# A gated-linear-attention layer: the six level products of a head as 64 by 64 products in one run, and a new order behind the merge

## The chip, the cores and the metric

The kernel runs on one core of one Trainium2 chip. The metric is the device time of one execution in microseconds. Three executions of the kernel before took 2208.63, 2210.24 and 2212.44 us; the median is 2210.24 us.

## The reference

One hybrid decoder layer over 2048 tokens plus 16 learned meta tokens, model width 1024, float32. One input projection feeds two branches, a Mamba-2 state-space branch (SSD, 16 heads in 4 groups, chunks of 128) and gated linear attention (GLA, 4 heads, key width 128, value width 256). The branches are normalised, projected, gated by sigmoids, summed, projected once more and added to the residual; a last RMS norm follows. The change touches only the attention matrix of GLA inside a chunk:

```python
def step(s, inp):                      # one chunk of one GLA head
    qi, ki, vi, gi = inp               # gi: cumulative sum of log gates
    o_inter = einsum('bhtk,bhkv->bhtv', qi * exp(gi), s)
    rel = exp(where(causal, gi[:, :, :, None, :] - gi[:, :, None, :, :], -inf))
    att = einsum('bhtk,bhsk,bhtsk->bhts', qi, ki, rel)
    o_intra = einsum('bhts,bhsv->bhtv', att, vi)
    k_dec = ki * exp(gi[:, :, -1:] - gi)
    s_new = exp(gi[:, :, -1])[..., None] * s + einsum('bhsk,bhsv->bhkv', k_dec, vi)
    return s_new, o_inter + o_intra
```

## The kernel before, in words

**Stages.** The 2048 tokens are four blocks of 512 (`BLK`). For each block the first stage walks through 48 to 49 pieces of projection work on TensorE (PE); most pieces are 24 products of 512 columns or 48 of 256 on PE. After each piece `step()` lets every running generator go one step: `ssd_scan` for the four SSD groups, `gla_scan` for the four GLA heads, `gates`, `fetch_u` for the next block. In this text GLA heads are counted through, 0 to 15, four a block: head 9 is the second head of the third block. A second stage, after all blocks, does the branch and output projections.

**Who sets the order.** In the first stage PE and the DMA queue of SyncE run in program order, written out by hand. VectorE (DVE), ScalarE (ACT) and GpSimd (POOL) are put in order by a scheduler when the kernel is built; on the chip each runs its list in order. `tc.issue_after(x)` is a wish to that scheduler: what is inside comes behind `x` on `x`'s engine. Tiles come from pools: a tag with `bufs=n` has n slots, and a tile has to wait for a slot until the last reader of the tile in it is done.

**One GLA head** (`gla_scan`, L814 on). A chunk of 128 by 128 attention is put together from levels. For the half sizes 64, 32, 16, 8, 4, 2 (`LEVELS`) `level_in` (L847) computes scaled keys and queries: a subtraction on DVE (L858), two exponentials on ACT (L861, L862), and three products on DVE (L863 for the keys, L865 twice for the queries) into the tile `kq`. `level_out` (L869) multiplies them on PE, two products of 128 by 128 (L873), into a PSUM bank of the pool `pc` (two banks), and puts the part that belongs to the level into `xa`: ACT copies the first (L877), DVE copies the others under a mask (L880). The levels of one head are spread over four steps. In step five comes the last level, the sums for the pairs next to each other and the diagonal (L945, PE, by a matrix of ones), and the merge on DVE: L947 under a mask into `xa`, L950 times the triangles into `att`, L953 the diagonal under a mask. In step six PE transposes half of `att` (L960) and `advance(0)` adds the first two chunks to the state: six products on PE, then two updates on DVE (L969). In step seven PE computes the output of chunks 0 and 1 (L981 and three products each), and `advance(2)`, which takes the PSUM bank that `advance(0)` had and so must wait until both updates have read it. The next head begins at step seven of this one, so its levels stand beside them.

In the last block heads 13 and 14 begin closer to each other: head 14 is begun at the end of `proj_v12` (`LATE_G`), and where two scans run in these steps the newer one goes first.

**Slots.** `sq` has six slots (`ex`, `kq` and `att` of GLA, the decay matrices of SSD), `c1` eight, `xd` four.

**SSD's products inside a chunk** (L717) already have the form that the change brings to GLA: stationary 64 columns of `dm`, moving 64 columns of `xdt`, output rows 0 to 63 and 64 to 127 in turn.

Of the kernel before, what the change touches and what calls it, by code (L numbers as in the profile page):

```python
# [8 lines left out]
F32 = mybir.dt.float32  # L9
# [10 lines left out]
BLK = 512  # L20
NCH = BLK // P
# [2 lines left out]
NH = 16  # L24
EPS = 1e-6
NWR = 3
NSQ = 6
NT4 = 5
NACT = 8
NC1 = 8  # L30
NAS = 6
LATE_G = 2
LEVELS = (64, 32, 16, 8, 4, 2)
# [10 lines left out]
def trunk_kernel(ctx: ExitStack, tc: tile.TileContext, xm, xmt, w_feat, w_tok, w_v3, w_zm, w_br, w_o,  # L44
                 cf32, cmsk, pvec, fnw, hvec, gw2, out):
    nc = tc.nc
# [80 lines left out]
    bpool, wk, sm, const = pool1("bpool", 1), pool1("wk", 2), pool1("sm", 4), pool1("const", 1)  # L127
# [4 lines left out]
    pc = ctx.enter_context(tc.tile_pool(name="pc", bufs=2, space=bass.MemoryType.PSUM))  # L132
# [4 lines left out]
    def bank(pool, tag):  # L137
        return mk(pool, [P, 512], F32, tag)
# [5 lines left out]
    tris = cst[:, 2:4, :]  # L144
# [246 lines left out]
    msk = const.tile([P, NMSK, P], U8, name="msk")  # L391
# [225 lines left out]
            feats.append(f)  # L617
            yield

    cbs, evicted, convd = {}, [], []  # L620

    def behind():
        return tc.issue_after(evicted[-1].ins) if evicted else nullcontext()
# [6 lines left out]
    def ssd_scan(o, g):  # L630
# [10 lines left out]
        if m0:  # L641
            ps = bank(pt, "pt")
# [20 lines left out]
                                tri.unsqueeze(1).to_broadcast([P, NCH, P]), op=ALU.mult)  # L663
        yt = mk(wk, [P, NCH, 256], F32, "tok4", bufs=NT4)
        ssq = mk(sm, [P, 4], F32, "ssq")
        held, intra = {}, {}

        def before(c):
            a = m0 + c * P
            ci = ci0 + c  # L670
            if c + 1 < NCH:
                fetch_cb(o, g, c + 1)
            cb = cbs.pop((g, c))
            ps = bank(pt, "pt")
            for j, f in enumerate((x0, x1, bf)):
                nc.tensor.transpose(ps[:, j * P:(j + 1) * P], f[:, a:a + P], ident)
            px = ps[:, :256].rearrange("p (h c) -> p h c", c=64)
            xdt = mk(wk, [P, 4, 64], F32, "xd", bufs=NCH)
            nc.vector.tensor_tensor(xdt, px, hb(tkd[:, ci, hs], P), op=ALU.mult)
            xw = mk(wk, [P, 4, 64], F32, "c1", bufs=NC1)  # L680
            nc.vector.tensor_tensor(xw, px, hb(wde[:, ci, hs], P), op=ALU.mult)
            nc.vector.tensor_tensor(yt[:, c].rearrange("p (h c) -> p h c", c=64), px,
                                    hb(d_skip[:, hs], P), op=ALU.mult)
            bt = mk(wk, [P, P], F32, "bt")
            nc.scalar.activation(bt, ps[:, 256:384], AF.Copy)
            dm = mk(wk, [P, 4, P], F32, "sq", bufs=NSQ)
            with behind() if o.b == 0 else nullcontext():
                for h in range(4):
# [58 lines left out]
        r = rstd_of(ssq, 4, 1.0 / 1024)  # L747
# [63 lines left out]
    def gla_scan(o, h, last=False):  # L811
# [27 lines left out]

        xa = mk(wk, [P, 2, P], F32, "c1", bufs=NC1)
        kqs = {}

        def level_in(half):
            nb = BLK // (2 * half)
            npc = P // (2 * half)  # L847

            def view(t):
                return t.rearrange("p (b two h) -> p b two h", two=2, h=half)  # L850

            def view5(t):
                return t.rearrange("p (r o b two h) -> p r o b two h", o=2, b=npc, two=2, h=half)

            ex = mk(wk, [P, BLK], F32, "sq", bufs=NSQ)
            kq = mk(wk, [P, BLK], F32, "sq", bufs=NSQ)
            ev = view(ex)
            nc.vector.tensor_tensor(  # L858
                ex.rearrange("p (b s) -> p b s", s=2 * half), gr.rearrange("p (b s) -> p b s", s=2 * half),
                view(gr)[:, :, 0, half - 1:half].to_broadcast([P, nb, 2 * half]), op=ALU.subtract)  # L860
            nc.scalar.activation(ev[:, :, 0], ev[:, :, 0], AF.Exp, scale=-ITEMP)  # L861
            nc.scalar.activation(ev[:, :, 1], ev[:, :, 1], AF.Exp, scale=ITEMP)  # L862
            nc.vector.tensor_tensor(view(kq)[:, :, 0], ev[:, :, 0], view(k)[:, :, 0], op=ALU.mult)  # L863
            for i in range(2):
                nc.vector.tensor_tensor(view5(kq)[:, :, 1 - i, :, 1], view5(ex)[:, :, i, :, 1],  # L865
                                        view5(q)[:, :, i, :, 1], op=ALU.mult)
            kqs[half] = kq

        def level_out(half):  # L869
            kq = kqs.pop(half)  # L870
            ps = bank(pc, "pc")
            for r in range(2):
                nc.tensor.matmul(ps[:, r * P:(r + 1) * P], kq[:, 2 * r * P:(2 * r + 1) * P],  # L873
                                 kq[:, (2 * r + 1) * P:(2 * r + 2) * P], start=True, stop=True)
            pv2 = ps[:, :256].rearrange("p (r t) -> p r t", t=P)
            if half == 64:
                nc.scalar.activation(xa, pv2, AF.Copy)  # L877
            else:
                mi = msk[:, LEVELS.index(half)].unsqueeze(1).to_broadcast([P, 2, P])
                nc.vector.copy_predicated(xa, mi, pv2)  # L880

        level_in(64)
        yield
        if m0:
            ps = bank(pt, "pt")
# [12 lines left out]
        if not last:  # L898
            turn_keys()
        level_in(32)  # L900
        level_out(64)
        level_in(16)
        yield
        if m0:
            ps = bank(pt, "pt")
            nc.tensor.matmul(ps[:, :256], btm[:META], s_gla[:META, h], start=True, stop=True)
            nc.vector.tensor_copy(s_gla[:, h], ps[:, :256])
        level_out(32)
        level_in(8)
        level_out(16)  # L910
        level_in(4)
        yield
        level_out(8)
        level_in(2)
        level_out(4)


        def halves(t):
# [18 lines left out]
        yield  # L937
        if last:
            turn_keys()
        level_out(2)  # L940
        sums_ = []
        for hl, n in parts:
            ps = bank(pt, "pt")
            for i in range(2):
                nc.tensor.matmul(ps[:, :n], ones_r, hl[i], start=i == 0, stop=i == 1)  # L945
            sums_.append(ps)
        nc.vector.copy_predicated(xa, msk[:, len(LEVELS)].unsqueeze(1).to_broadcast([P, 2, P]),  # L947
                                  sums_[0][:, :256].rearrange("p (r t) -> p r t", t=P))
        att = mk(wk, [P, NCH, P], F32, "sq", bufs=NSQ)
        nc.vector.tensor_tensor(att.rearrange("p (r o) t -> p r o t", o=2),  # L950
                                xa.unsqueeze(2).to_broadcast([P, 2, 2, P]),
                                tris.unsqueeze(1).to_broadcast([P, 2, 2, P]), op=ALU.mult)
        nc.vector.copy_predicated(att, msk[:, 0].unsqueeze(1).to_broadcast([P, NCH, P]),  # L953
                                  sums_[1].rearrange("p (c t) -> p c t", t=P))
        atp = [beside_64("atp") for _ in range(2)]
        split(*[t[:, 0::2] for t in atp], att[:, 0::2])
        yield
# [548 lines left out]
def _layout(inputs):  # L1506
# [40 lines left out]
    cmsk[:, 0] = np.eye(P)  # L1547
    for i, h in enumerate(LEVELS + (1,)):
        if i:
            cmsk[:, i] = (row // (2 * h) == col // (2 * h)) & (row // h != col // h)  # L1550

    def pcol(v):
        return v.reshape(-1, P).T
# [37 lines left out]
```

## Time and profile before

The profiled execution took 2209.51 us; the trace spans 2207.7 us of it, from the first instruction to the last.

| engine | busy us | share of the span | instructions |
|---|---|---|---|
| PE, matmuls | 2174.5 | 98% | 12301 |
| PEld, weight loads (beside PE) | 1867.9 | 85% | 12301 |
| DVE | 1553.8 | 70% | 2871 |
| ACT | 1188.5 | 54% | 2767 |
| POOL | 693.8 | 31% | 689 |

A row of the timeline reads: start us, duration us, engine, line, operation, out<-in, partitions x elements, count, and in brackets how long the engine was idle before and what it waited for. PE's matmuls overlap each other, so the time that a matmul takes up is the distance between two starts, not its duration. The same holds, by less, on DVE. A float32 matmul stands in the trace as two records.

### The profile page before, as it was taken

To read this page: it belongs to the slowest core of one execution; us is meant where nothing else is said; L and a number is where in the kernel's file an instruction comes from. 1 tells how busy PE (TensorE), PEld (TensorE's weight loads), DVE (VectorE), ACT (ScalarE), POOL (GpSimd) and SP (SyncE) were. 2 spreads that over 40 slices of the span, in tenths; PEclk is the share of its full clock that TensorE was granted. 3 is DMA by queue.
4 is the path that set the end of the run, shared out by engine and by line. 5 is a ranking of instruction groups with operands and counts; after the bars stand their busy time and mean duration, and the time that the engine had idled before them with its cause. 6 is when DMAs were issued, how large, how long until landed. Compare 5 with 4: busy or idle time off the path is not lost.

```text
span 2207.7 us, 35845 instructions
## 1 busy us (share of the span) xinstructions
PE 2174.5 (98%) x12301; PEld 1867.9 (85%) x12301; DVE 1553.8 (70%) x2871; ACT 1188.5 (54%) x2767; POOL 693.8 (31%) x689
## 2 busy tenths in 40 slices
PE   7999999999999999999999999999999999999998
PEld 7999889888888988888988888878888888888887
DVE  5786675677577676658677666674789955789876
ACT  5666655466455456545465554464644545554544
POOL 5444433222222122221222100166233374324341
PEclk9999999999999999999999999999999999999999
DMA  9766775667778677778677664376768866787753
GB/s 316 254 228 235 255 271 211 218 217 244 257 253 265 210 227 230 249 257 274 208 223 238 215 216 161 124 265 214 246 221 297 304 223 216 240 286 255 255 187 121
DMA packets 313702, 518.00 MB, mean 235 GB/s; under 512 B 28080, under 2 KB 162480, under 8 KB 313520
## 3 DMA queue, kind: packets, MB, share of 16 engines
q1 hardware_dynamic: 247008, 419.89, 58.3%
q10 hardware_dynamic: 65872, 93.74, 11.6%
q8 instruction: 96, 1.57, 0.3%
q0 software_dynamic: 640, 2.10, 0.2%
q14 instruction: 86, 0.70, 0.1%
HBM read 368.42 MB, written 147.19 MB: 234 GB/s over the span
## 4 chain that ended last, share of the span: by engine, by line
PE 86%; DVE 4%; ACT 3%; DMA 3%; POOL 1%; issue 1%; SPq 1%; POOLq 0%; ACTq 0%; DVEq 0%
PE pj L223 19%; PE pj L225 19%; PE pj L224 19%; PE pt L225 4%; PE pt L224 4%; PE pt L223 4%; PE pc L223 2%; PE pc L224 2%; PE pc L225 2%; PE pc L873 2%; PE pc L717 1%; PE pc L701 1%; PE pc L981 1%; PE pc L700 1%; DVE acc L612 1%
## 5 line engine op out<-in xcount | busy, mean ns | idle before, releaser
L223 PE MATMUL pj<-ue,whl 128*128 128x512 f32 (+2 forms) x672 | 236.7, 352 | 2.3 <-ACT acc L608 2.2
L224 PE MATMUL pj<-ue,whl 128*128 128x512 f32 (+2 forms) x672 | 228.9, 341 | 0.0
L225 PE MATMUL pj<-ue,whl 128*128 128x512 f32 (+2 forms) x672 | 228.5, 340 | 0.0
L223 PE MATMUL pj<-uo,whl 128*128 128x512 f32 x512 | 206.0, 402 | 0.0
L225 PE MATMUL pj<-uo,whl 128*128 128x512 f32 x512 | 199.9, 390 | 0.0
L224 PE MATMUL pj<-uo,whl 128*128 128x512 f32 x512 | 199.5, 390 | 0.0
L223 PE MATMUL pj<-b,a 128*128 128x512 f32 (+1 forms) x484 | 187.4, 387 | 0.5 <-DVE io L1304 0.5
L224 PE MATMUL pj<-b,a 128*128 128x512 f32 (+1 forms) x484 | 187.4, 387 | 0.0
L225 PE MATMUL pj<-b,a 128*128 128x512 f32 (+1 forms) x484 | 187.4, 387 | 0.0
L612 DVE SCALAR_TENSOR_TENSOR acc<-cin,hcw,acc 128x512 f32<-128x512 f32 (+1 forms) x192 | 156.1, 813 | 29.2 <-ACT acc L608 27.5
L1157 POOL TENSOR_TENSOR as<-ar,ar 128x512 f32<-128x512 f32 x38 | 58.3, 1534 | 371.4 <-DMA ar<-in_w_br 124.7
L83 POOL TENSOR_TENSOR wr<-wr 128x256 f32<-128x256 f32 x80 | 69.7, 871 | 332.2 <-DMA wr<-y 142.0
L1186 DVE TENSOR_TENSOR a<-ar,a 128x512 fp32r<-128x512 f32 x160 | 132.1, 834 | 58.8 <-ACT a L1185 57.8
L223 PEld LDWEIGHTS pj<-ue,whl 128*128 128x128 f32 x672 | 127.2, 189 | 18.3 <-ACT acc L608 3.1
L186 POOL TENSOR_TENSOR whl<-wr,whl 128x512 fp32r<-128x512 f32 (+1 forms) x76 | 102.6, 1357 | 122.0 <-ACT whl L184 93.4
L225 PEld LDWEIGHTS pj<-ue,whl 128*128 128x128 f32 x672 | 127.1, 189 | 14.4
L224 PEld LDWEIGHTS pj<-ue,whl 128*128 128x128 f32 x672 | 127.7, 190 | 13.3
L1186 DVE TENSOR_TENSOR a<-as,a 128x512 fp32r<-128x512 f32 x120 | 104.8, 875 | 41.5 <-ACT a L1185 38.2
L1185 ACT ACTIVATE a<-ar 128x512 fp32r<-128x512 f32 x160 | 99.1, 626 | 58.6 <-PE pt L225 22.1
L1220 ACT ACTIVATE sn<-pj 128x512 f32<-128x512 f32 x118 | 70.2, 595 | 110.8 <-PE pj L225 71.0
L224 PE MATMUL pt<-b,a 128*128 128x512 f32 x320 | 124.5, 389 | 0.0
L225 PE MATMUL pt<-b,a 128*128 128x512 f32 x320 | 124.5, 389 | 0.0
(335 smaller groups left out, 6367.9 us busy)
## 6 DMA issues: line engine op xcount, KB each, us to landing
whl<-k_s SPq DMA_DIRECT2D x96, 512.0 KB, 4.1
whl<-k_g SPq DMA_DIRECT2D x96, 512.0 KB, 4.5
whl<-k_v SPq DMA_DIRECT2D x36, 512.0 KB, 3.8
wr<-in_w_feat SPq DMA_DIRECT2D x64, 256.0 KB, 4.1
k_s<-whl SPq DMA_DIRECT2D x32, 512.0 KB, 3.8
cb<-cumd SPq DMA_DIRECT2D x64, 256.0 KB, 4.7
y<-gg ACTq DMA_DIRECT2D x64, 256.0 KB, 4.2
k_g<-whl SPq DMA_DIRECT2D x32, 512.0 KB, 3.7
```

The costliest lines, as they stand in the source:

```text
L83: nc.gpsimd.tensor_tensor(o, x, y, op=ALU.subtract)
L186: nc.gpsimd.tensor_tensor(hl[:, 1], raw, hl[:, 0].bitcast(F32), op=ALU.subtract)
L223: nc.tensor.matmul(ps, sh, mh, start=first, stop=False, **kw)
L224: nc.tensor.matmul(ps, sh, ml, start=False, stop=False, **kw)
L225: nc.tensor.matmul(ps, sl, mh, start=False, stop=last, **kw)
L612: convd[:] = [nc.vector.scalar_tensor_tensor(acc, cin[:, k:k + tt], hcw[:, ti, k:k + 1], acc, op0=ALU.mult, op1=ALU.add)]
L700: nc.tensor.matmul(ps[:, :256], cf[:, a:a + P], s_ssd[:, g], start=True, stop=True)
L873: nc.tensor.matmul(ps[:, r * P:(r + 1) * P], kq[:, 2 * r * P:(2 * r + 1) * P], kq[:, (2 * r + 1) * P:(2 * r + 2) * P], start=True, stop=True)
L1157: nc.gpsimd.tensor_tensor(s1, a21, a22, op=ALU.add)
L1185: nc.scalar.activation(t[:, 0], src, AF.Copy)
L1186: latest[:] = [nc.vector.tensor_tensor(t[:, 1], src, t[:, 0].bitcast(F32), op=ALU.subtract)]
L1220: nc.scalar.activation(sn, self.ps[n, "a"], AF.Copy)
```

## The change

The level products become four products of 64 by 64 for each level (two pairs of chunks, two halves of the chunk), one on output rows 0 to 63 and one on rows 64 to 127; the parts of 128 by 128 that the mask threw away are not computed. For level 64 the halves are crossed, for the others they lie on the diagonal. All six levels of a head go out in one run, in step five, into two banks of `pc` (four levels in one, two in the other). `xa` becomes a tile of its own, half as wide. Level 64 goes from PSUM right into two quarters of `att` on ACT, GpSimd zeroes the other two; level 32 is copied into `xa` on ACT, levels 16, 8, 4 and 2 under a mask on DVE, half as wide as before. The merge works on quarters (two masked copies and two products where there was one each) and then puts in the diagonal as before. `level_in(64)` of the next head is issued behind the last merge that the program has come to. `kq` gets six slots of its own, shared with SSD's `xdt` and `dm`; `sq` goes to three, `c1` to six.

```diff
-NSQ = 6
+NSQ = 3
+NKQ = 6
-NC1 = 8
+NC1 = 6
...
-            xdt = mk(wk, [P, 4, 64], F32, "xd", bufs=NCH)
+            if c % 2 == 0:
+                pair[:] = [mk(wk, [P, 2, 4, 64], F32, "kq", bufs=NKQ)]
+            xdt = pair[0][:, c % 2]
...
-            dm = mk(wk, [P, 4, P], F32, "sq", bufs=NSQ)
+            dm = mk(wk, [P, 4, P], F32, "kq", bufs=NKQ)
...
-        xa = mk(wk, [P, 2, P], F32, "c1", bufs=NC1)
+        xa = mk(wk, [P, 2, 64], F32, "xa", bufs=1)
...
-            kq = mk(wk, [P, BLK], F32, "sq", bufs=NSQ)
+            kq = mk(wk, [P, BLK], F32, "kq", bufs=NKQ)
...
-        def level_out(half):
-            kq = kqs.pop(half)
-            ps = bank(pc, "pc")
-            for r in range(2):
-                nc.tensor.matmul(ps[:, r * P:(r + 1) * P], kq[:, 2 * r * P:(2 * r + 1) * P],
-                                 kq[:, (2 * r + 1) * P:(2 * r + 2) * P], start=True, stop=True)
-            pv2 = ps[:, :256].rearrange("p (r t) -> p r t", t=P)
-            if half == 64:
-                nc.scalar.activation(xa, pv2, AF.Copy)
-            else:
-                mi = msk[:, LEVELS.index(half)].unsqueeze(1).to_broadcast([P, 2, P])
-                nc.vector.copy_predicated(xa, mi, pv2)
-
-        level_in(64)
+        quads = [(slice(i * 64, i * 64 + 64), slice(j * 64, j * 64 + 64)) for i, j in ((0, 0), (1, 1))]
+
+        def levels_out(att):
+            ps = [bank(pc, "pc").rearrange("p (l r t) -> p l r t", r=2, t=64) for _ in range(2)]
+            pl = [ps[n // 4][:, n % 4] for n in range(len(LEVELS))]
+            for n, half in enumerate(LEVELS):
+                kq = kqs.pop(half)
+                for r in range(2):
+                    for i in range(2):
+                        j = 1 - i if half == 64 else i
+                        nc.tensor.matmul(pl[n][i * 64:i * 64 + 64, r],
+                                         kq[:, 2 * r * P + i * 64:2 * r * P + i * 64 + 64],
+                                         kq[:, (2 * r + 1) * P + j * 64:(2 * r + 1) * P + j * 64 + 64],
+                                         start=True, stop=True)
+            for i in range(2):
+                rows, off = slice(i * 64, i * 64 + 64), slice(64 - i * 64, P - i * 64)
+                nc.scalar.activation(att[rows, i::2, off], pl[0][rows], AF.Copy)
+                nc.gpsimd.memset(att[rows, 1 - i::2, off], 0.0)
+            nc.scalar.activation(xa, pl[1], AF.Copy)
+            for n in range(2, len(LEVELS)):
+                nc.vector.copy_predicated(xa, msk[:, n, :64].unsqueeze(1).to_broadcast([P, 2, 64]), pl[n])
+
+        with tc.issue_after(merged[-1].ins) if merged else nullcontext():
+            level_in(64)
...
-        level_out(2)
+        att = mk(wk, [P, NCH, P], F32, "sq", bufs=NSQ)
+        levels_out(att)
...
-        nc.vector.copy_predicated(xa, msk[:, len(LEVELS)].unsqueeze(1).to_broadcast([P, 2, P]),
-                                  sums_[0][:, :256].rearrange("p (r t) -> p r t", t=P))
-        att = mk(wk, [P, NCH, P], F32, "sq", bufs=NSQ)
-        nc.vector.tensor_tensor(att.rearrange("p (r o) t -> p r o t", o=2),
-                                xa.unsqueeze(2).to_broadcast([P, 2, 2, P]),
-                                tris.unsqueeze(1).to_broadcast([P, 2, 2, P]), op=ALU.mult)
-        nc.vector.copy_predicated(att, msk[:, 0].unsqueeze(1).to_broadcast([P, NCH, P]),
-                                  sums_[1].rearrange("p (c t) -> p c t", t=P))
+        near = sums_[0][:, :256].rearrange("p (r t) -> p r t", t=P)
+        for rows, on in quads:
+            nc.vector.copy_predicated(xa[rows], msk[rows, len(LEVELS), :64].unsqueeze(1).to_broadcast([64, 2, 64]),
+                                      near[rows, :, on])
+        for rows, on in quads:
+            nc.vector.tensor_tensor(att[rows, :, on].rearrange("p (r o) t -> p r o t", o=2),
+                                    xa[rows].unsqueeze(2).to_broadcast([64, 2, 2, 64]),
+                                    tris[rows, :, on].unsqueeze(1).to_broadcast([64, 2, 2, 64]), op=ALU.mult)
+        merged[:] = [nc.vector.copy_predicated(att, msk[:, 0].unsqueeze(1).to_broadcast([P, NCH, P]),
+                                               sums_[1].rearrange("p (c t) -> p c t", t=P))]
```

The other four calls of `level_out`, between the calls of `level_in`, are gone, and the masks on the host are made for a width of 64.

**What moves on PE.** This is PE's list before around step five of head 9: the end of a projection piece, the last level's product, the sums, the next piece.

```order
L225 MATMUL pj_12225<-ue_8700,whl_12240 128x512
L873 MATMUL pc_12270<-sq_12196 128x128 x2
L945 MATMUL pt_12274<-c_2146_12217,ones_r 128x256
L945 MATMUL pt_12274<-c_2147_12218,ones_r 128x256
L945 MATMUL pt_12277<-sq_12221,ones_r 128x512
L945 MATMUL pt_12277<-sq_12222,ones_r 128x512
L223 MATMUL pj_12288<-ue_8141,whl_12289 128x512
```

And this is the same place in the changed kernel (its lines are numbered a little higher: L226 is the third product of a projection group, L882 the level product, L954 the sums).

```order
L226 MATMUL pj_12298<-ue_8762,whl_12313 128x512
L882 MATMUL pc_12344<-kq_12054 64x64 x4
L882 MATMUL pc_12344<-kq_12124 64x64 x4
L882 MATMUL pc_12344<-kq_12132 64x64 x4
L882 MATMUL pc_12344<-kq_12184 64x64 x4
L882 MATMUL pc_12345<-kq_12192 64x64 x4
L882 MATMUL pc_12345<-kq_12273 64x64 x4
L954 MATMUL pt_12379<-c_2081_12290,ones_r 128x256
L954 MATMUL pt_12379<-c_2082_12291,ones_r 128x256
L954 MATMUL pt_12382<-sq_12294,ones_r 128x512
L954 MATMUL pt_12382<-sq_12295,ones_r 128x512
```

The five earlier products of the head have left the steps before and stand here; apart from that PE's list in the first stage is as it was, and SyncE's is the same throughout.

**What moves on DVE, head 9, behind `advance(0)`.** Before, from the first state update (L969, `c_2170`) to the second, which frees the bank for `advance(2)`, there stand the gate (L803), a split (L273) and two steps of the next head's levels (L863, L858).

```order
L969 SCALAR_TENSOR_TENSOR c_2170_12341<-s_gla,egl_11954,pc_12334 128x256 [waits PE_49]
L803 SCALAR_TENSOR_TENSOR gg_12317<-gg_12317,pj_12288 128x512 [waits Activation_49]
L273 TENSOR_TENSOR atp_12285<-pt_12329,atp_12284 128x2x128 [waits Activation_49]
L863 TENSOR_TENSOR sq_12515<-sq_12514,act_11819 128x16x16 [waits Activation_49]
L858 TENSOR_TENSOR sq_12591<-g_all_9056 128x512
L969 SCALAR_TENSOR_TENSOR c_2171_12343<-c_2170_12341,egl_11954,pc_12334 128x256 [waits DVE_49]
```

In the changed kernel the updates are L980, and between them stand a split (L274), a subtraction of the next head (L861), a low part of the next block's input (L357) and two whole levels of the next head (L866, L868).

```order
L980 SCALAR_TENSOR_TENSOR c_2106_12447<-s_gla,egl_12047,pc_12440 128x256 [waits PE_49]
L274 TENSOR_TENSOR atp_12391<-pt_12435,atp_12390 128x2x128 [waits Activation_49]
L861 TENSOR_TENSOR sq_12697<-g_all_9131 128x512 [waits DVE_49]
L357 TENSOR_TENSOR uo_12491<-acc_12488,uo_12491 128x512 [waits Activation_49]
L866 TENSOR_TENSOR kq_12617<-sq_12616,act_11912 128x16x16 [waits Activation_49]
L868 TENSOR_TENSOR kq_12617<-sq_12616,act_11818 128x2x4x16 [waits Activation_49]
L868 TENSOR_TENSOR kq_12617<-sq_12616,act_11818 128x2x4x16
L866 TENSOR_TENSOR kq_12690<-sq_12689,act_11912 128x32x8 [waits Activation_49]
L868 TENSOR_TENSOR kq_12690<-sq_12689,act_11818 128x2x8x8 [waits Activation_49]
L868 TENSOR_TENSOR kq_12690<-sq_12689,act_11818 128x2x8x8
L980 SCALAR_TENSOR_TENSOR c_2107_12449<-c_2106_12447,egl_12047,pc_12440 128x256 [waits DVE_49]
```

Between the merge's last copy and the first update the list has grown too: before, six instructions of the next head's levels and two subtractions L858 stand there, now six and four subtractions L861, and the gate L806, which stood behind the update.

**What moves on DVE, head 13.** Before, the merge of head 13 (L880 for level 2, L947, L950, L953) is one piece, with one subtraction of head 14 in it.

```order
L865 TENSOR_TENSOR sq_15966<-sq_15965,act_15483 128x2x4x16
L880 COPY_PREDICATED c_2794_15632<-msk,pc_15973 128x256 [waits PE_49]
L947 COPY_PREDICATED c_2794_15632<-msk,pt_15977 128x256 [waits DVE_49,PE_49]
L950 TENSOR_TENSOR sq_15984<-c_2794_15632,cst 128x512 [waits DVE_49]
L858 TENSOR_TENSOR sq_16028<-g_all_12831 128x512 [waits PE_49]
L953 COPY_PREDICATED sq_15984<-msk,pt_15980 128x512 [waits DVE_49,PE_49]
```

In the changed kernel `kq_15993` is head 13's level 2, `kq_16071` and `kq_16079` are levels of head 14, `xa_15769` is head 13's. `kq` has six slots; when `kq_15993` asks for one, five hold head 13's other levels and one holds head 14's level 64, so it gets the slot of head 13's level 64 (both have the same address), and waits for PE to have read that.

```order
L866 TENSOR_TENSOR kq_15993<-sq_15992,act_15385 128x128x2 [waits PE_49]
L868 TENSOR_TENSOR kq_15993<-sq_15992,act_15318 128x2x32x2 x2
L274 TENSOR_TENSOR sq_16015<-sq_16008,sq_16014 128x512 [waits DVE_49]
L861 TENSOR_TENSOR sq_16070<-g_all_12950 128x512 [waits DVE_49]
L861 TENSOR_TENSOR sq_16078<-g_all_12950 128x512 [waits PE_49]
L866 TENSOR_TENSOR kq_16071<-sq_16070,act_15674 128x8x32 [waits Activation_49]
L868 TENSOR_TENSOR kq_16071<-sq_16070,act_15587 128x2x2x32 [waits Activation_49]
L868 TENSOR_TENSOR kq_16071<-sq_16070,act_15587 128x2x2x32
L892 COPY_PREDICATED xa_15769<-msk,pc_16087 128x128 [waits Activation_49]
L866 TENSOR_TENSOR kq_16079<-sq_16078,act_15674 128x16x16 [waits Activation_49]
L861 TENSOR_TENSOR sq_16170<-g_all_12950 128x512 [waits DVE_49]
L868 TENSOR_TENSOR kq_16079<-sq_16078,act_15587 128x2x4x16 [waits Activation_49]
```

It goes on like this: from L861 of `sq_16078` to the merge's last copy (L964) stand 30 DVE instructions: 4 masked copies of levels (L892), 2 of the sums (L958), 2 products (L961), the last copy, and between them for head 14 three more subtractions (L861) and all of levels 32, 16, 8 and 4, two instructions of level 2 (five L866 and nine L868 in all), L939 (its q times k), and L834 and L839 for head 15. Head 14's `level_in(64)` had been issued behind head 12's merge, the last one that the program had come to.

More of the change, by code (lines that the diff above doesn't have):

```diff
@@ L618, in proj_conv @@
             yield
-    cbs, evicted, convd = {}, [], []
+    cbs, evicted, convd, merged = {}, [], [], []
     def behind():
@@ L665, in ssd_scan @@
         ssq = mk(sm, [P, 4], F32, "ssq")
-        held, intra = {}, {}
+        held, intra, pair = {}, {}, []
         def before(c):
@@ L900, in gla_scan @@
         level_in(32)
-        level_out(64)
         level_in(16)
@@ L907, in gla_scan @@
             nc.vector.tensor_copy(s_gla[:, h], ps[:, :256])
-        level_out(32)
         level_in(8)
-        level_out(16)
         level_in(4)
         yield
-        level_out(8)
         level_in(2)
-        level_out(4)
         def halves(t):
@@ L1549, in _layout @@
         if i:
-            cmsk[:, i] = (row // (2 * h) == col // (2 * h)) & (row // h != col // h)
+            near = (row % 64 // (2 * h) == col // (2 * h)) & (row % 64 // h != col // h)
+            cmsk[:, i] = near & (col < 64)
     def pcol(v):
```

## Prediction

> **What bounds the kernel now.** I read the page's engine row first, then the chain, then the view of what each engine waited for.
>
> ```profile
> PE 2174.5 (98%) x12301; PEld 1867.9 (85%) x12301; DVE 1553.8 (70%) x2871; ACT 1188.5 (54%) x2767; POOL 693.8 (31%) x689
> ...
> PE 86%; DVE 4%; ACT 3%; DMA 3%; POOL 1%; issue 1%; SPq 1%; POOLq 0%; ACTq 0%; DVEq 0%
> ...
> PE pc L223 <- DVE c L969: 2.8, 3, 2.1
> ```
>
> PE is busy for 98% of the span and holds 86% of the chain that ends it. So a product that PE need not do is worth its whole time, and a wait that PE did not have costs its whole time. PE waits for the state updates (L969) three times, 2.8 us in all: little, but this is the narrow place of GLA.
>
> **What goes: the 128 by 128 products.** A level product stands in the trace as two records. Three places of PE's timeline give both prices.
>
> ```profile
> 671.36 0.39 PE L224 MATMUL pt<-whl,uo 128*128 128x512 f32 x1
> 671.59 0.39 PE L225 MATMUL pt<-whl,uo 128*128 128x512 f32 x1
> 671.82 1.05 PE L873 MATMUL pc<-sq 128*128 128x128 f32 x8
> 672.62 0.48 PE L223 MATMUL pj<-whl,uo 128*128 128x512 f32 x1
> 672.94 0.40 PE L224 MATMUL pj<-whl,uo 128*128 128x512 f32 x1
> ...
> 524.78 0.39 PE L225 MATMUL pj<-uo,whl 128*128 128x512 f32 x1
> 525.10 2.09 PE L717 MATMUL pc<-xd,sq 128*64 128x64 f32 x64
> 527.12 0.50 PE L223 MATMUL pj<-uo,whl 128*128 128x512 f32 x1
> 527.45 0.39 PE L224 MATMUL pj<-uo,whl 128*128 128x512 f32 x1
> ...
> 525.32 1.40 PE L717 MATMUL pc<-xd,sq 128*64 128x64 f32 x42
> ```
>
> Eight old records: from 671.59 to 672.94 are 1.35 us; two neighbours of 0.23 each (671.36 to 671.59) leave 0.90, or 0.112 a record. A head has 24 records: 2.69 us. SSD's L717 has the new form already. Its 64 records: 527.45 - 524.78 = 2.67, less two neighbours, 2.22 us. In the middle, 42 records last 1.40; less some 0.22 for one record that is 1.18 over 20 distances, 0.059 for each two records. A new head has 48 records, 16 fewer than L717: 2.22 - 8 x 0.059 = **1.75 us**. The saving is 0.94 a head, **15.0 us** for 16 heads.
>
> The edges are in this price: the step into L717's run is 525.10 - 524.78 = 0.32 where 0.23 is usual, and the step behind 527.12 again 0.33. [...]
>
> **What this does to PE's timetable.** At the last level the new run takes 1.75 us where one old level took 4 x 0.112 = 0.45. So what follows on PE comes 1.30 later, counted from the start X of that run.
>
> **The merge.** It gets longer: ACT's copies, then on DVE four masked copies, two more, two products, the diagonal. A 128-wide masked copy isn't in the trace. A dependent 256-wide one takes 0.48 from its start to the next (1372.04 to 1372.52, below) and two independent 128-wide products 0.40 (1375.29 to 1375.69): 0.20 to 0.48 are my bounds. I take 0.38 in a chain, nearer the upper end since each copy waits for the one before, and 0.25 among others. ACT's new copies lie between nothing and the 0.39 of the old one. First masked copy at X + 1.7, four of them 1.5, two more 0.65, products 0.85, diagonal 0.75: att is ready at X + 5.5.
>
> ```profile
> 1027.96 0.60 PE L873 MATMUL pc<-sq 128*128 128x128 f32 x4
> ...
> 1033.17 0.73 DVE L953 COPY_PREDICATED sq<-msk,pt 128x512 f32<-128x512 uint8 x1
> ...
> 1034.57 0.38 PE L960 MATMUL pt<-cst,sq 128*128 128x128 f32 x2
> ...
> 1042.45 0.47 DVE L969 SCALAR_TENSOR_TENSOR c<-c,egl,pc 128x256 f32<-128x256 f32 x1
> ...
> 1042.97 0.39 PE L223 MATMUL pc<-tok,kdt 128*128 128x256 f32 x1 [0.27 <-DVE c L969]
> ```
>
> PE asks for att (L960) at X + 6.6 here before, a piece behind the sums, and so at X + 7.9 now. The piece hides the longer merge, and the memsets, in most heads.
>
> **Head 9, the second update.** In these rows the second L969 ends at 1042.92, and PE, which needs the bank, waits 0.27. The new list puts two whole levels of the next head in front of it. Price by starts in DVE's rows: subtraction L858 0.60, L863 0.33, L865 0.20; the gate and L357, as wide as L858, 0.60 too. PE is there at 1042.97 - 0.27 = 1042.70.
>
> ```profile
> 1372.04 0.45 DVE L947 COPY_PREDICATED c<-msk,pt 128x256 f32<-128x256 uint8 x1
> 1372.52 0.69 DVE L950 TENSOR_TENSOR sq<-c,cst 128x512 f32<-128x512 f32 x1
> 1373.13 0.68 DVE L858 TENSOR_TENSOR sq<-g_all 128x512 f32<-128x512 f32 x1
> 1373.73 0.73 DVE L953 COPY_PREDICATED sq<-msk,pt 128x512 f32<-128x512 uint8 x1
> 1374.36 0.41 DVE L863 TENSOR_TENSOR sq<-sq,act 128x256 f32<-128x256 f32 x1
> 1374.69 0.69 DVE L858 TENSOR_TENSOR sq<-g_all 128x512 f32<-128x512 f32 x1
> 1375.29 0.49 DVE L865 TENSOR_TENSOR sq<-sq,act 128x128 f32<-128x128 f32 x2
> 1375.69 0.42 DVE L273 TENSOR_TENSOR atp<-sq,atp 128x256 fp32r<-128x256 f32 x1
> ```
>
> From merge to first update: two more subtractions and the gate, less L357, +1.2; between the updates +1.2 (0.60 + 0.60 + 2 x 0.73 now against 0.60 + 0.33 + 0.60, the split on both sides). Before, from the merge's end (1033.90) to the second update's end were 9.0; now 11.4. The merge here stands behind a gate that ACT delivers late, so I take its end at X + 7.0: the update ends at X + 18.4. PE is there at 1042.70 - 1027.96 + 1.30 = X + 16.0. Wait 2.4, added **2.1**.
>
> Heads 0, 1 and 5 go the same way. Head 0 waited 2.07 already; its list to the second update grows from 7.5 to 8.7 us of work: **+1.1**. Head 1 had 2.25 us to spare (PE starts `advance(2)` at 353.12, the update ended at 350.87) and gets 3.1 us more work and a merge 1 later, against 1.3 later on PE and 0.6 saved by the subtraction that leaves the merge: 3.1 + 1.0 - 1.3 - 0.6 - 2.25 = 0.0. I count **+1.1** (0 to 2.2), one stop, because in block 0 DVE stands still while POOL works (the last two rows):
>
> ```profile
> 350.40 0.47 DVE L969 SCALAR_TENSOR_TENSOR c<-c,egl,pc 128x256 f32<-128x256 f32 x1
> ...
> 353.12 0.28 PE L223 MATMUL pc<-tok,kdt 128*128 128x256 f32 x1
> ...
> 343.74 1.34 POOL L186 TENSOR_TENSOR whl<-wr,whl 128x512 fp32r<-128x512 f32 x1 [2.51 <-ACT whl L184]
> ...
> 343.85 1.38 DVE L865 TENSOR_TENSOR sq<-sq,act 128x128 f32<-128x128 f32 x1
> ```
>
> (1.38 for an instruction that takes 0.28 elsewhere, so a stop costs 1.1.) Head 5: **+0.4**. Heads 2, 6 and 10 had 4.8 to spare and keep about 1.5; 4, 8 and 12 likewise; in 3, 7 and 11 nothing of a next head stands there.
>
> **Heads 13 and 14, the merge itself.** Here heads overlap and the six slots bind: level 2 of head 13 can only be written when PE has read level 64, within the run. That alone is nothing: about 0.9 us of DVE beside 1.2 of PE. But DVE then walks through head 14's levels between the pieces of head 13's merge. The 30 instructions that end with the diagonal, by the starts above: 4 subtractions 2.4, five L866 1.7, nine L868 1.8, L939, L834 and L839 1.8 (0.60 each, 512 wide), masked copies 1.5, products 0.7, diagonal 0.6: 10.5 us. They begin when the sums have been read, X + 2.7, so att is ready at X + 13.2.
>
> ```profile
> 1370.85 0.48 PE L945 MATMUL pt<-c,ones_r 128*128 128x256 f32 x2
> ...
> 1371.63 0.39 PE L223 MATMUL pj<-uo,whl 128*128 128x512 f32 x1
> ...
> 1377.08 1.05 PE L873 MATMUL pc<-sq 128*128 128x128 f32 x8
> ```
>
> PE: run 1.75, sums 0.78 (1370.85 to 1371.63), piece 5.45 (1371.63 to 1377.08, where a level of head 14 stood and goes): it asks at X + 8.0 and waits **5.2** (4.3 to 5.7 with the copies' bounds). Behind PE stand head 13's state and all of the next pieces. In head 14 the same count (23 instructions, 8.4 us from X + 2.4) gives X + 10.8 against X + 9.6: **+1.2**. Head 15, with half a piece for cover: **+0.3**.
>
> **The clock.** PE's idle time has a second price.
>
> ```profile
> 106.66 0.38 PE L223 MATMUL pj<-whl,ue 128*128 128x256 f32 x1 [2.06 <-ACT acc L608]
> ...
> 232.94 0.55 PE L676 MATMUL pt<-cst,act 128*128 128x128 f32 x3 [2.44 <-ACT s_gla L785]
> ...
> 305.10 0.46 PE L223 MATMUL pc<-tok,kdt 128*128 128x256 f32 x1 [2.07 <-DVE c L969]
> ...
> 107.80:111.20 3.40, 3.40 (x20) 0.57 0.23 82
> 234.10:237.50 3.40, 3.40 (x11) 0.57 0.80 264
> 305.80:309.20 3.40, 3.40 (x19) 0.58 0.65 226
> ```
>
> Behind each of the three waits over 2 us the granted clock is 0.57 for 3.4 us, some 1.5 us lost. Head 13 pays that: **+1.5**. Head 9, at 2.4, may: I count half, **+0.8**. [...]
>
> **The sum.** -15.0 + 2.1 + 1.1 + 1.1 + 0.4 + 5.2 + 1.2 + 0.3 + 1.5 + 0.8 = **-1.3 us** on the profiled 2209.51 (span 2207.7): 2208.2. The median of the runs shown is 0.7 higher; on it the forecast is **2209 us**, no change. A measurement of this kernel can tell about 0.2%, 4.4 us, from none. Nothing else moves on PE in the first stage; the shorter `sq` and `c1` rings are free where their tiles live one or two steps.
>
> **The rivals.**
> 1. *The gain stays.* DVE is only 70% busy, and my chains add small prices. If only head 13's wait comes (4.3 to 5.2, clock 1.5) and the rest falls into slack, 8 to 10 us remain: 2200 to 2202; with a short wait there too, 2198. Against it: the wait of head 13 follows from the order itself.
> 2. *Slower: the second update is late in more heads.* It decides where merge to second update takes over 11 us on DVE. Heads 2, 6, 10, 4 and 8 come to 9 to 10 by my prices; one or two stops for POOL of 1.1 each push them over. Then each costs 1 to 2 us, and the windows at half clock in heads 1 and 9 come too: +6 to +12, 2214 to 2221. For it: DVE had no idle time from merge to update in heads 1, 4 and 9. Against it: POOL works on only 31% of the span.
> 3. *The change doesn't do what it says:* the halves don't run side by side, since here each half has its own moving columns and in L717 both have the same. Then 48 records at 0.059 and the edges are 3.2 us a head, 0.5 more than before: +8 for -15, about 2231. [...]
>
> ```profile
> 525.05:527.20 2.15, 2.09 (x64) 1.95 (x64) 0.69 (x1) 0.00 (x0) 1.00 0.76 257
> ```
>
> **How the numbers follow.** Forecast (2205 to 2214): 0.50. Rival 1: 0.27. Rival 2: 0.20. Rival 3: 0.03. So faster by over 0.2% 0.27, within 0.50, slower 0.23. The range takes in the forecast, most of rival 1 and the lower part of rival 2: 2199 to 2217.
>
> **What would show it.** L882 should stand as 768 records, a run of 48 taking about 1.75 us with its edges; if over 2.7, rival 3. PE should wait once for about 5 us at the transposes (L971) for DVE's L964 near the end of the first stage, with the clock at half behind it, and some 2 us each for L980 in heads 0, 1 and 9. If the 5 us are missing, rival 1; if L980 stands with many heads, rival 2. The forecast is wrong if other waits appear, above all between ACT and the new copies.

## The result, and the profile after

The changed kernel takes **2234.43 us** (median of 4, 2232.68 to 2238.13), the kernel before 2211.34 beside it: ratio 1.0109, interval 1.0093 to 1.0125. It is slower, by 23 to 24 us, and outside the range of 2199 to 2217. The profiled execution took 2232.68 us with a span of 2230.9; before it was 2207.7, so the traces differ by 23.2 us.

The page of the changed kernel, engine row and chain:

```profile
PE 2168.9 (97%) x12685; PEld 1852.2 (83%) x12685; DVE 1544.2 (69%) x2887; ACT 1193.3 (53%) x2799; POOL 721.1 (32%) x721
...
PE 70%; DVE 8%; DMA 4%; ACT 2%; POOL 1%; issue 1%; ACTq 0%; SPq 0%; POOLq 0%; DVEq 0%
```

PE's work shrank as intended, and yet PE holds 70% of the chain instead of 86%; DVE has 8 instead of 4. What PE waited for, in the changed kernel (us in total, times, longest):

```profile
PE pt L971 <- DVE sq L964: 15.5, 9, 6.1
...
PE pc L224 <- DVE c L980: 4.9, 3, 2.4
PE pt L499 <- ACT sq L490: 4.1, 3, 1.9
PE pj L224 <- DVE gg L806: 2.8, 3, 0.9
PE pc L226 <- DVE atp L274: 2.6, 2, 1.6
...
PE pc L703 <- DVE s_ssd L707: 2.2, 2, 1.1
```

Before, L964's twin L953 did not stand in this list. All waits of PE together were 25.2 us before and are 54.1 now, **+28.9**. Stretches at half clock follow many of the waits (start and end of a window, its length, PE, loads, DVE, ACT and POOL busy, granted clock, DMA share, GB/s):

```profile
107.80:111.20 3.40, 3.40 (x18) 3.40 (x18) 3.40 (x7) 2.90 (x9) 1.43 (x2) 0.50 0.16 56
234.10:237.50 3.40, 3.36 (x17) 2.88 (x18) 1.98 (x7) 1.93 (x4) 2.36 (x3) 1.00 0.77 257
298.00:301.40 3.40, 3.40 (x14) 3.08 (x15) 3.40 (x11) 3.31 (x9) 0.00 (x0) 0.62 0.89 282
463.30:466.70 3.40, 3.40 (x10) 2.42 (x11) 2.86 (x5) 2.99 (x6) 0.19 (x1) 0.66 0.30 102
705.80:709.20 3.40, 3.40 (x13) 2.82 (x14) 3.40 (x8) 3.03 (x9) 0.00 (x0) 0.64 0.23 89
1055.50:1058.90 3.40, 3.40 (x12) 3.03 (x13) 3.40 (x9) 3.02 (x9) 0.00 (x0) 0.58 0.22 83
1397.00:1400.40 3.40, 3.40 (x20) 3.40 (x21) 2.99 (x7) 1.73 (x5) 0.00 (x0) 0.61 0.00 0
```

The first stretch was there before (107.80 in the prediction) and is twice as long now; the two others of before are gone (234.10 has a clock of 1.00 here, and head 0's second update hardly waits now); six are new, the five other rows at 0.58 to 0.66 and one from 1464 on. What a stretch costs is put here as 1 minus the clock, times the time that PE is busy in it, an estimate: products of 512 columns start 0.43 us apart at a clock of 0.50 (464.97 to 465.40) and 0.23 apart at 1.00 (468.61 to 468.84). Added up over windows of 0.2 us that is 5.1 us before and 12.3 now, **+7.2**. By the distances between starts, the products cost 43.2 us before and 28.2 now: **-15.0**. That makes +21.1 of 23.2; what is left, 2.1 us, is 0.11 us for each of 19 more waits if it belongs to them, which was not tried apart.

### Where the merge stands now

For each head, counted from the start X of the run (before: of the last level's product), when the merge's last copy ends, and when PE has reached the transposes, its own wait taken off:

| head | before: merge / PE | after: merge / PE | after: what stood in front |
|---|---|---|---|
| 1, 2, 6, 10, 12 | 3.6 to 4.5 / 6.6 | 6.0 / 7.8 | nothing |
| 0 | 6.6 / 6.8 | 12.0 / 8.0 | the gate (ACT, DVE), L352 |
| 4, 8 | 3.6 / 7.5 | 9.3 / 8.9 | the gate on ACT |
| 5, 9 | 4.6, 5.9 / 6.6 | 6.8, 7.2 / 7.8 | the next block's input (ACT L355) and the gate |
| 3, 7, 11 | 4.2 to 4.4 / 6.6 | 8.1 to 8.6 / 8.0 | SSD's L613 and L617 |
| 13 | 4.4 / 7.9 | 14.1 / 8.2 | levels of head 14 |
| 14 | 3.6 / 8.6 | 11.1 / 10.3 | levels of head 15 |
| 15 | 3.6 / 3.9 | 6.9 / 5.2 | a split of keys (L273, L274); half a piece for cover |

ACT and DVE in head 4 of the changed kernel, X = 642.71:

```profile
640.15 0.33 ACTq L762 DMA_DIRECT2D y<-gg  x1
645.84 0.60 ACT L805 ACTIVATE gg<-pj 128x512 f32<-128x512 f32 x1 [5.71 <-DMA y<-gg]
646.33 0.59 ACT L769 ACTIVATE act<-pj 128x512 f32<-128x512 f32 x1
646.81 0.56 ACT L888 ACTIVATE sq<-pc 64x128 f32<-64x128 f32 x2
647.40 0.28 ACT L890 ACTIVATE xa<-pc 128x128 f32<-128x128 f32 x1
...
646.47 0.69 DVE L806 SCALAR_TENSOR_TENSOR gg<-gg,pj 128x512 f32<-128x512 f32 x1 [7.46 <-ACT gg L805]
647.71 1.38 DVE L892 COPY_PREDICATED xa<-msk,pc 128x128 f32<-128x128 uint8 x4 [0.55 <-ACT xa L890]
649.19 0.63 DVE L958 COPY_PREDICATED xa<-msk,pt 64x128 f32<-64x128 uint8 x2
649.85 1.30 DVE L961 TENSOR_TENSOR sq<-xa,cst 64x256 f32<-64x256 f32 x2
651.29 0.72 DVE L964 COPY_PREDICATED sq<-msk,pt 128x512 f32<-128x512 uint8 x1
```

The gate's tile `gg` (four slots, shared with SSD's output `yo`) waits until `yo`'s DMA, issued at 640.15, has landed: 5.7 us. The merge's first copies (L888, L890) are now on ACT, behind that gate, so the merge begins at X + 4.1, where it begins at X + 1.2 in head 1 with nothing in front. Before, ACT's part of the merge was done three steps earlier. The gate waited for the same DMA then too, and the merge (X = 642.28) ended in time all the same:

```profile
641.52 0.60 ACT L802 ACTIVATE gg<-pj 128x512 f32<-128x512 f32 x1 [3.14 <-DMA y<-gg]
...
645.17 0.74 DVE L953 COPY_PREDICATED sq<-msk,pt 128x512 f32<-128x512 uint8 x1
```

### The profile page after: what moved, and what is told of

Same layout as the page of the kernel before. It is cut to its first block, busy times and chain, and to the rows that moved or that the text cites. A ratio compares the mean times of both kernels' runs of the same rounds, so it can differ in the third digit from the quotient of the medians.

```text
span 2230.9 us, 36746 instructions
## 1 busy us (share of the span) xinstructions
PE 2168.9 (97%) x12685; PEld 1852.2 (83%) x12685; DVE 1544.2 (69%) x2887; ACT 1193.3 (53%) x2799; POOL 721.1 (32%) x721
## 4 chain that ended last, share of the span: by engine, by line
PE 70%; DVE 8%; DMA 4%; ACT 2%; POOL 1%; issue 1%; ACTq 0%; SPq 0%; POOLq 0%; DVEq 0%
PE pj L224 15%; PE pj L226 15%; PE pj L225 15%; PE pt L226 4%; PE pt L225 4%; PE pt L224 4%; PE pc L224 2%; PE pc L225 2%; PE pc L226 2%; DVE sq L861 1%; PE pc L720 1%; PE pc L703 1%; DMA y<-gg 1%; PE pc L704 1%; DVE kq L868 1%
## 5 line engine op out<-in xcount | busy, mean ns | idle before, releaser
L226 PE MATMUL pj<-ue,whl 128*128 128x512 f32 (+2 forms) x672 | 228.0, 339 | 0.0
L226 PE MATMUL pj<-uo,whl 128*128 128x512 f32 x512 | 201.3, 393 | 0.0
L226 PE MATMUL pj<-b,a 128*128 128x512 f32 (+1 forms) x484 | 187.4, 387 | 0.0
L1168 POOL TENSOR_TENSOR as<-ar,ar 128x512 f32<-128x512 f32 x38 | 64.0, 1683 | 366.5 <-DMA ar<-in_w_br 167.5
L613 DVE SCALAR_TENSOR_TENSOR acc<-cin,hcw,acc 128x512 f32<-128x512 f32 (+1 forms) x192 | 155.8, 811 | 29.6 <-ACT acc L609 28.2
L226 PEld LDWEIGHTS pj<-ue,whl 128*128 128x128 f32 x672 | 126.7, 189 | 14.3
L226 PE MATMUL pt<-b,a 128*128 128x512 f32 x320 | 124.3, 389 | 0.0
```

What stands on the lines that cost most here:

```text
L226: nc.tensor.matmul(ps, sl, mh, start=False, stop=last, **kw)
L613: convd[:] = [nc.vector.scalar_tensor_tensor(acc, cin[:, k:k + tt], hcw[:, ti, k:k + 1], acc, op0=ALU.mult, op1=ALU.add)]
L1168: nc.gpsimd.tensor_tensor(s1, a21, a22, op=ALU.add)
```

## The experiments

Theory **M**: the one run leaves the whole merge behind it, on ACT and DVE in turn, with too little cover. Theory **R**: the new rings (`sq` three, `kq` six and shared with SSD) move other work, in SSD and around the state. Theory **I**: the wish that puts `level_in(64)` of the next head behind the merge crowds DVE just there.

**e1, without the wish.**

```diff
-        with tc.issue_after(merged[-1].ins) if merged else nullcontext():
+        if True:
             level_in(64)
```

> The changed kernel, except that level_in(64) of the next head is no longer issued behind the merge. In the changed kernel's profile (2232.7 us) PE waits 15.5 us at the transposes L971 for the merge (L964), 4.9 for the second update (L980), 2.8 for the gate (L806), 2.6 for the split (L274), 4.1 for L490 of the gates. Theory M (the merge begins only when the one run ends, and its chain ACT copies - masked copies - quarters is too long for its cover): the L971 waits stay at 12 to 18 us, time 2228 to 2238. Theory I (the wish puts the next head's first level between the merge and what PE waits for): L980, L806 and L274 waits go, 2215 to 2222. Theory R (the shared and shorter rings): no change, 2230 to 2236.

Ratio to before 1.0242 (1.0227 to 1.0257), 2264.33 us: 30 us slower than the changed kernel. What PE waited for:

```profile
PE pt L971 <- DVE sq L964: 53.7, 15, 12.9
```

No theory expected this size, and I points the wrong way. In head 0 of this run DVE has seven instructions of the next head's levels between the first masked copies (L892) and the sums' copies (L958), all of them behind in the changed kernel. The wish keeps them out; it is what makes one run bearable.

**e2, the wish alone in the kernel before.**

```diff
+        with tc.issue_after(merged[-1].ins) if merged else nullcontext():
-        level_in(64)
+            level_in(64)
```

> The kernel before, with only the wish added: level_in(64) of the next head issued behind the last merge. Theory I: slower by 5 to 12 us (2216 to 2223), with new waits at L969. Theories M and R: within 3 us of before (2208 to 2214).

Ratio 0.9988 (0.9976 to 1.0000): no loss, though one wait of 2.6 us at L960 appears in head 0. With e1, theory I falls.

**e3, two runs a head.** `levels_out(att, 0)` does levels 64 to 8 with ACT's copies and two masked copies at the start of step four, `levels_out(att, 1)` levels 4 and 2 in step five.

```diff
         yield
+        att = mk(wk, [P, NCH, P], F32, "kq", bufs=NKQ); levels_out(att, 0)
         level_in(2)
...
-        att = mk(wk, [P, NCH, P], F32, "sq", bufs=NSQ)
-        levels_out(att)
+        levels_out(att, 1)
```

> The changed kernel with the products of a head in two runs: levels 64, 32, 16, 8 with ACT's copies and two masked copies in step four, levels 4 and 2 in step five; att takes a slot of kq. PE pays a second pair of edges: by L717's prices 2.07 for 1.75 us, and the part before the sums is shorter; at most +0.33 a head, +5 us in all. Theory M: the merge after the sums is some 2 us shorter and no longer stands behind ACT, so most of the 15.5 us at L971 goes with its half-clock windows: 2218 to 2226. Theories I and R: 2234 to 2240, waits at L980, L806, L490 as in the changed kernel.

Ratio 1.0042 (1.0027 to 1.0057), 2219.76 us, 15 less than the changed kernel. The runs cost 1.28 + 0.81 = 2.09 us a head, 33.4 in all, 5.2 more than one run, so the waits that went, with what came behind them, were worth 20:

```profile
PE pt L971 <- DVE kq L964: 5.5, 3, 3.3
PE pj L224 <- ACT acc L609: 4.9, 3, 2.9
PE pt L499 <- ACT sq L490: 3.8, 3, 1.9
PE pc L224 <- DVE c L980: 3.6, 4, 1.5
PE pc L703 <- DVE s_ssd L707: 3.3, 3, 1.1
```

L971 fell from 15.5 to 5.5 (head 13 from 6.1 to 1.2; head 0 keeps 3.3), while L499 stayed and L703 grew from 2.2 to 3.3. Theory M holds for the first, and leaves R the second.

**e4, the rings alone in the kernel before.**

```diff
-NSQ = 6
+NSQ = 3; NKQ = 6
-NC1 = 8
+NC1 = 6
...
-            xdt = mk(wk, [P, 4, 64], F32, "xd", bufs=NCH)
+            if c % 2 == 0: pair[:] = [mk(wk, [P, 2, 4, 64], F32, "kq", bufs=NKQ)]
+            xdt = pair[0][:, c % 2]
-            dm = mk(wk, [P, 4, P], F32, "sq", bufs=NSQ)
+            dm = mk(wk, [P, 4, P], F32, "kq", bufs=NKQ)
-            kq = mk(wk, [P, BLK], F32, "sq", bufs=NSQ)
+            kq = mk(wk, [P, BLK], F32, "kq", bufs=NKQ)
```

> The kernel before, with only the new rings: kq with six slots for GLA's levels and SSD's xdt and dm, sq three, c1 six (xa stays in c1, so c1 is one slot tighter than in the changed kernel). Theory R: 6 to 12 us slower (2217 to 2223) with waits at L498 for L489 (4 us in the changed kernel) and in head 13. Theories M and I: within 3 us of before (2208 to 2214).

Ratio 1.0059 (1.0043 to 1.0074), 2225.17 us: **+13 us** with not one product changed.

```profile
PE pc L223 <- DVE c L970: 7.0, 5, 2.1
...
PE pt L498 <- ACT sq L489: 3.4, 3, 1.4
PE pc L701 <- DVE s_ssd L705: 3.3, 3, 1.1
```

The second updates of heads 5 and 9 (L970 here) wait 2.08 and 1.87 us, in the same places as in the changed kernel (2.35 and 2.36). Head 13, where waits were expected too, has hardly any. L498 waits where L499 does there, and the order on ACT shows why. First the kernel before, then the changed one, then e4, at the same place of the second block:

```profile
459.94 0.98 ACT L689 ACTIVATE sq<-cb,tkc 128x128 f32<-128x128 f32 x3
...
460.83 0.57 ACT L489 ACTIVATE sq<-pt 16x512 fp32r<-16x512 f32 x1
...
462.12 1.70 ACT L993 ACTIVATE ot<-ot,rstd 128x256 f32<-128x256 f32 x4
```

```profile
461.04 0.91 ACT L1004 ACTIVATE ot<-ot,rstd 128x256 f32<-128x256 f32 x2 [1.01 <-POOL rstd L269]
...
461.85 0.89 ACT L1004 ACTIVATE ot<-ot,rstd 128x256 f32<-128x256 f32 x2
462.65 0.57 ACT L490 ACTIVATE sq<-pt 16x512 fp32r<-16x512 f32 x1
```

```profile
461.59 1.31 ACT L994 ACTIVATE ot<-ot,rstd 128x256 f32<-128x256 f32 x3 [0.41 <-POOL rstd L268]
...
462.80 0.49 ACT L994 ACTIVATE ot<-ot,rstd 128x256 f32<-128x256 f32 x1
463.20 0.57 ACT L489 ACTIVATE sq<-pt 16x512 fp32r<-16x512 f32 x1
```

With the old rings ACT works ahead on SSD's decay matrices (L689) and the scheduler puts the gates' L489, for which PE waits next, in front of the four scalings of GLA's output. With the short rings no decay matrices stand here, and the scalings come first, in e4 as in the changed kernel. One of them waits for POOL (1.01 us in the changed kernel, 0.41 in e4), and PE waits 1.86 us there for L490 and 0.84 in e4 for L489. That the scheduler had too few slots to work ahead is the likely reason, not one that a run shows. Some of the 13 us lies outside the first stage: 2.2 us are waits for L1221 in the second stage, for which there was no row before.

**e5, two runs and the old kind of rings.** On e3: one ring `sq` of seven for `ex`, `kq`, `att` and `dm`, and `xdt` in `xd` again.

```diff
-NSQ = 3
-NKQ = 6
+NSQ = 7
...
-            if c % 2 == 0:
-                pair[:] = [mk(wk, [P, 2, 4, 64], F32, "kq", bufs=NKQ)]
-            xdt = pair[0][:, c % 2]
+            xdt = mk(wk, [P, 4, 64], F32, "xd", bufs=NCH)
```

> Two runs a head as in e3_two_runs (2219.8 us), with the rings of before as far as they fit: one ring sq of seven slots for ex, kq, att and SSD's dm, SSD's xdt in xd with four slots again; c1 stays at six, xa its own tile. Theory R: the waits for L490 (3.8 us) and L707 (3.3, of which before had 1.9 for another reason) go, the second updates (L980, 3.6) get smaller: 8 to 13 us less than e3, 2207 to 2212, about before. Theory M alone (rings do nothing): 2218 to 2222. If the seven slots now bind GLA's levels, L971 or L882 waits appear instead and the time is 2222 or more.

Ratio 0.9993 (0.9981 to 1.0005), 2207.33 us: 0.0049 or 11 us less than e3. The waits at L499 and for L707 are gone, L980 is at 1.2 us. Theory R holds, at about the size of e4. New is a wait of 3.8 us at L882 for the levels, in the first heads of the later blocks (4, 8 and 12). In head 8 ACT waits twice for `yo`'s DMA shortly before the exponentials (L864):

```profile
976.43 0.69 ACT L761 ACTIVATE gg<-pt,hsw 128x512 f32<-128x512 f32 x1 [2.49 <-DMA y<-gg]
...
979.38 0.60 ACT L805 ACTIVATE gg<-pj 128x512 f32<-128x512 f32 x1 [1.00 <-DMA y<-gg]
979.87 0.43 ACT L864 ACTIVATE sq<-sq 128x256 f32<-128x256 f32 x1
```

**e6, e5 without the wish** (the diff of e1).

> As e5_two_runs_old_rings, without the wish that puts level_in(64) behind the merge. If the wish is needed because the next head's levels get between the sums and the merge (e1: 53.7 us at L971), L971 waits grow and it is 10 us or more slower than e5; if that came from the long merge and the six slots of kq alone, it is within 4 us of e5.

Ratio 1.0194 (1.0181 to 1.0208), 33.4 us at L971 in 11 waits. The wish is needed with the shorter merge and the long ring as well. Why the kernel before does not need it was not tried apart.

**e7, `yo` out of `gg`** (on e5), and **e8, the same from the second block on.**

```diff
-            yo = mk(wk, [P, BLK], F32, "gg", bufs=4)
+            yo = mk(wk, [P, BLK], F32, "sq", bufs=NSQ)
```

> As e5_two_runs_old_rings, with SSD's output tile yo (its DMA to DRAM has to land before the slot is free) in a slot of sq, no longer of gg. In the changed kernel the gate's ACT step L805 waits in heads 0, 4 and 8 for that DMA (3.4, 5.7 and 5.6 us idle before it) and the merge's copies stand behind it. If that is what is left at L971 (5.5 us in e3, 3.3 of it in head 0), it is 3 to 6 us faster than e5; if the copies of step four are early enough, no change (within 2 us); if the DMA now holds a slot that the levels need, slower.

> As e7_y_off_gg (2201.6 us), but in the first block yo stays in gg. In e7 PE waits once 2.4 us at L954 in head 0, for a split of the diagonal whose sq slot came late, with 0.9 us at half clock behind it; in e5 (yo in gg throughout) head 0 waits nowhere. If yo's DMA holds that slot: 2 to 4 us faster than e7, 2198 to 2200. If not: as e7.

e7: 0.9965 (0.9953 to 0.9976), 2201.55 us. e8: 0.9952 (0.9938 to 0.9965), **2198.35 us, 10.8 us faster than before** and the fastest here. The waits for the levels at L882 fall to 0.3 us in both: with the gate no longer waiting for a DMA, ACT's exponentials come in time. So e7's size was as expected, but not its place: of the waits at L971 e5 had only 0.7 us left. In e8 the 2.4 us at L954 of e7 are gone, as expected; the intervals of the two overlap. What PE waited for in e8:

```profile
PE pt L334 <- DMA cst<-in_cf: 9.2, 1, 9.2
PE pt L677 <- ACT s_gla L788: 4.3, 1, 4.3
PE pj L224 <- ACT acc L609: 4.1, 3, 2.1
PE pt L971 <- DVE sq L964: 1.7, 2, 1.0
```

All waits of PE in e8 sum to 25.0 us, as many as before (25.2). Its products cost 33.9 us for 43.2: 9.3 saved. The saving in products now arrives whole in the time, within the interval (7.7 to 13.7 us).

**e9, `yo` out of `gg` in the changed kernel** (the diff of e7, with a slot of `kq`).

> The changed kernel (one run, short rings), only with SSD's yo in a slot of kq, no longer of gg. Theory M in the form that the merge of heads 0, 4 and 8 is late because ACT's copies stand behind the gate, which waits for yo's DMA: the L971 waits of these three heads (4.1, 0.6, 0.6 us) and the splits behind them in 4 and 8 (2.6) go, 5 to 9 us faster than the changed kernel, 2224 to 2229; the waits in 7, 11, 13, 14, 15 stay. If the length of the chain alone makes them late: no change, 2231 to 2236.

Ratio 1.0129 (1.0112 to 1.0146): no gain in all, where 5 to 9 us were expected, but both halves can be seen. In heads 4 and 8 the merge ends at X + 6.0 and 6.4 instead of 9.3, and their waits at L971 are gone, as that form of M says. In head 0 the DMA now holds a slot of `kq`: the next `yo` waits 4.1 us for it on ACT, the gate and the splits stand behind, and a new wait of 8.1 us at L954 comes of it. Head 9 has a new one of 1.3 us at L971.

```profile
291.23 0.69 ACT L761 ACTIVATE kq<-pt,hsw 128x512 f32<-128x512 f32 x1 [4.09 <-DMA y<-kq]
```

So the gate was the cause in heads 4 and 8; moving the DMA into a ring that is full gives it back.

**e10, the slots of e4 in one ring** (`sq` of nine in the kernel before, pairs of `xdt` and `c1` of six as in e4).

> The kernel before, with the same number of slots as e4_rings_only (2225 us), but in one ring: sq of nine for ex, kq, att, dm and the pairs of xdt; c1 six. Theory R as a matter of splitting one ring into two short ones: the waits at L498 (3.4 us) and most of those at L970 (7.0) go, 2210 to 2217. If what costs is that xdt lives in pairs of two chunks, or c1 of six: as e4, 2219 to 2227.

Ratio 1.0018 (1.0005 to 1.0031), 2212.63 us. L498 has no row, L970 fell from 7.0 to 0.9; the waits for L705 (4.2) stay, and one of 4.5 us at L961, for the exponential L863, is new in head 0. So most of e4's loss, some 9 of 13 us, comes from cutting one ring into two short ones. What is left, 4 us, is the pairs, `c1` and the new order together; they were not tried apart.

## Why the prediction was wrong, by its own steps

- **The products** were right: 1.75 us a run forecast, 1.75 measured in 15 of 16 heads; 15.0 saved forecast, 15.0 measured. What follows the sums on PE came 1.30 later, as forecast. The 48 records of a run took 1.75 us, not the 3.2 of rival 3, so rival 3 is out. (The window under rival 3 is L717's run: products busy 2.09 and weight loads 1.95 of 2.15 us.)
- **The rings** are the first step that failed: "the shorter `sq` and `c1` rings are free where their tiles live one or two steps". e4 puts them at +13 us. The step asked only whether a tile would find a slot, and PE's order had not changed; what changed was the order that the scheduler gave ACT and DVE in SSD and around the state, without a new wait for a slot showing in the trace (in e4 DVE waits 8.5 us for PE in front of L864, the first product into a level's tile, and 18.7 before in front of its twin L863). PE's list being "as it was" says nothing of the engines that it waits for.
- **The merge's cover** is the second. Its length was nearly right (X + 5.5 forecast, X + 6.0 where nothing stands in front), and so was the time at which PE asks (7.9 and 7.8). But "The piece hides the longer merge, and the memsets, in most heads" took only what is inside the merge. With 1.8 us to spare, a gate behind a DMA on ACT (heads 0, 4, 8) or SSD's convolution on DVE (3, 7, 11) makes it late: 6.8 us of L971 waits in all (of 15.5; the others are in heads 13 to 15), 4.1 of them in head 0 with a half-clock stretch. Head 0 was forecast to wait 1.1 us more for its second update than the 2.07 of before; the merge was late first, and that update was then waited for 0.2 us.
- **Heads 13 to 15**: 5.2 forecast and 6.1 measured for head 13, with the stretch at half clock; 1.2 and 0.8 for head 14, with 0.6 more at L992; 0.3 and 1.8 for head 15, mis-sized. The order on DVE that the prediction read there is what the trace shows.
- **The second updates**: head 9 came as sized (2.4 and 2.36), head 5 at 2.35 for 0.4, head 1 not at all for 1.1. Head 9's list is longer as the prediction read it. But e4 has the waits of heads 5 and 9 without the wish and with the old products, so the rings alone are enough to make such lists. Head 9 was sized from its own list and came out; head 5 was not foreseen. (The difference between head 9's two lists is 1.13 us by the prices given, put as 1.2; it changes nothing.)
- **The clock** was mis-sized: 2.3 us in the sum, 7.2 measured, as waits that were not foreseen brought stretches of their own. Head 9 was counted at half and paid in full (0.58 in the row above, behind a wait of 2.36 us). A wait of 2.28 us at L677 paid nothing (1.00 in the row from 234.10), so that head 9 paid in full is luck.
- **Not foreseen at all**: 0.9 us for the gate L806 in heads 2, 6 and 10, and the splits L274 in heads 4 and 8 (2.6 us together), and, with the rings, 4.1 us at L499.

Rival 2 had the sign, but put it on more late second updates; only heads 5 and 9 had them. A kernel with the one run and one long ring would price the late merge alone. It was not tried, though one ring of nine, as in e10, takes no more room than the three and the six. So how the changed kernel's loss divides between the late merge and the rings rests on e3, e4 and e5, which each start from another kernel.

## What to carry to other kernels

Work that is moved together on the busiest engine moves its consumers together too: count how long the other engines need from the last product to the next one that needs them, and everything that may stand in front of it in their lists. A ring's size is an input to the scheduler even where the trace shows no new wait for a slot, so a change of slots should be timed alone. Here the same products in two runs, one shared ring, and a DMA's source out of the ring that a gate waits for turned 24 us lost into 11 us won.

## What the runs showed of the hardware

- Whether PE's clock halved behind a wait did not hang on the wait's length alone. In the changed kernel a wait of 1.77 us (head 15) and one of 2.28 us (L677) were followed by a granted clock of 1.00, one of 1.86 us in the second block by 0.66 (the windows of the last two stand above). In the kernel before one of 2.06 us was followed by 0.57.

```profile
1450.66 0.41 PE L971 MATMUL pt<-cst,sq 128*128 128x128 f32 x2 [1.77 <-DVE sq L964]
...
1451.00:1454.40 3.40, 3.40 (x27) 3.15 (x26) 3.36 (x8) 1.07 (x4) 2.43 (x2) 1.00 0.95 289
...
234.14 0.55 PE L677 MATMUL pt<-cst,act 128*128 128x128 f32 x3 [2.28 <-ACT s_gla L788]
...
463.27 0.72 PE L499 MATMUL pt<-sq,w 48*128 48x512 f32 x2 [1.86 <-ACT sq L490]
```

Read in windows of 0.2 us, the slow stretches of the changed kernel begin at 106.0, 297.2, 464.4, 706.8, 1054.9, 1392.9 and 1464.5 and last 3.4 or 6.8 us at a clock of 0.50. What else decides was not shown. For a forecast it means that a wait of some 2 us may cost a stretch at half clock or nothing.
- The same 256 KB DMA from `gg` took 3.0 to 4.7 us to land around 630 to 648 us before, and 5.6 to 6.0 after; 2.97 MB were moved between 634 and 646 us before, 3.60 MB between 636 and 648 us after. So the wait for this DMA was not a fixed price.
